# Two-layer latent backbone: attention norm weight, squares and high parts on ScalarE, norm product on GpSimd, and the last head's end in another order

## The chip, the cores and the metric

The kernel runs on one core of a Trainium2 chip. The metric is the device time of one execution in microseconds. A core has TensorE (PE in the profile; its weight loads are the row PEld), VectorE (DVE), ScalarE (ACT), GpSimd (POOL) and SyncE (SP), which issues nearly all DMAs from one queue. On-chip memory is SBUF; products land in PSUM, which has eight banks of 512 float32 columns here, and GpSimd is given no PSUM operand in this kernel.

## The reference

Two layers over 1024 latent tokens and 256 context tokens of 1024 channels: layer 0 is differential attention, layer 1 a state-space mixer, each followed by a squared-ReLU MLP, all in float32. The change touches layer 0's attention only:

```python
q_l = apply_rope(heads_qk(q_l), cos, sin) * scale          # 8 heads, 2 x 64 channels each
k_all, v_all = concatenate([k_c, k_l]), concatenate([v_c, v_l])   # 256 + 1024 keys
def attend(q, k, v):
    s = einsum('bqhcd,bkhcd->bhcqk', q, k)             # two maps c = 0, 1 per head
    p = softmax(s)
    w = p[:, :, 0] - lam * p[:, :, 1]
    o = einsum('bhqk,bkhe->bqhe', w, v)                    # 128 channels per head
    return rmsnorm(o, subln_g) * (1.0 - lambda_init)       # norm over the 128 channels, weight subln_g
y_lat = einsum('bte,ed->btd', o_l, w_o)                    # and y_ctx from the context alone
```

The context's queries read only the context's 256 keys.

## The kernel before

**Precision.** A float32 product is done as three matmuls on rounded halves: `mm3` (L132, L133, L134) multiplies high by high, high by low and low by high. The high part is a ScalarE copy into a rounded type, the low part the difference (`split`, L137 and L138; the low part on VectorE, or on GpSimd where so given).

**Phase B** (`phase_b`, about 220 to 876 us) does the attention of all eight heads. A head h has nine units: u = 0 is the 256 context queries, u = 1 to 8 are 128 latent queries each; step n = 9h + u. `with self.manual()` puts PE, VectorE, ScalarE and GpSimd in the order in which the program issues their instructions. SyncE's queue is not part of that: DMAs are placed by a scheduler once their operands are ready, and then run in the queue's order. In a unit:

- `scores` (L579): 18 matmuls (12 for u = 0) into PSUM columns 0 to 1279 and 1792 to 3071, for the two maps.
- `maxima` (L588 for u = 0, L592): VectorE copies the scores to SBUF with a running minimum.
- `exps` (L599, L602): ScalarE, in place, with the sum.
- `combine` (L610, L611, L613): VectorE, reciprocal, factor, and the difference of the two maps over 1280 columns (L613).
- In the next unit PE transposes the result (`w_part`, L620, L625) in parts w0 (four blocks), w1 (two), w2 (four). `w_direct` makes halves from PSUM: high on ScalarE (L631), low on VectorE (L632). `w_copy` frees PSUM first: a ScalarE copy to SBUF (L638), then high (L641) and low (L642) on GpSimd. The bank called `whole`, 1280 to 1791, shares banks with both maps' scores.
- Two units after an even u, `values` multiplies the halves of a pair of units by V into 256 columns of bank 6. `pair_out` copies the result (L732, ScalarE), squares it (L733, GpSimd, into `sq`), stores it to DRAM (`od`). `pair_sums` (L740) multiplies the squares by ones on PE.
- Between these PE works through `groups`: the q and k projections of the next head (`proj_group`; rotary product L534 on GpSimd, rotary add L537 on VectorE), and in head 7 the first part of the output product, `wo_group` (one 128-token tile over heads 0 to 5). A list of four numbers (`FILLS`, and for n from 63 on the tuple `a`) cuts the group's products into three fills between the other steps.
- **Norm.** At u 3 to 5 the statistics of the head before are finished (`norm_calc` L746 to L748, power on GpSimd L144, `norm_rows` writes rows `rsd`). At u 6, 7, 8 and the next head's 0, 1, `norm_load` brings one pair (values and broadcast row) from DRAM, and `norm_pair` in the same unit multiplies value, weight `self.sg` and row (L775, VectorE), splits it (ScalarE, GpSimd) and stores both halves (`on`). Two buffers take turns, for head 5 only one. For head 6 `norm6` (L796) does the same straight into the output product's operand `oT`; for head 7 `norm7` builds a diagonal matrix of the factors (L811, GpSimd), spreads it with ones on PE (L815) and multiplies (L817).
- **Turn to the output product.** From n = 62 `oT` takes the place of the projections' operand in the buffer H: `beside7` loads the stored halves of heads 0 to 5. `wload6` and `wsplit6` bring the output weights (n 57 to 62, and 72). `wo_group` (n 63 to 73) puts sums of six heads for each tile to DRAM (L858, `wod`); `wo_last` (n 74 to 76) does heads 6 and 7 for tiles 8, 9 and 0 to 4 into banks `WO_BANKS`, and the next phase does the rest.

In the main loop a unit takes one of two orders: with a pair to multiply that isn't pair 0 (or after u 0) the transposes come right after `values` (`late`; and `inside` where no group runs, u 4, 6, 8), otherwise there is a fill first.

Of the kernel before, what the change touches and what calls it, by code (L numbers as in the profile page):

```python
# [70 lines left out]
class Prog:  # L71
# [562 lines left out]
    def w_copy(self, tb, hi, lo):  # L634

        m, n = tb.shape[1:]
        t = shaped(self.wraw.next()[:, 0 : m * n], (m, n))
        self.nc.scalar.activation(t, tb, AF.Copy)  # L638

        def halves():  # L640
            self.nc.gpsimd.tensor_scalar(hi, t, 1.0, 0.0, ALU.mult, ALU.add)  # L641
            self.nc.gpsimd.tensor_tensor(lo, t, hi.bitcast(F32), ALU.subtract)  # L642

        return halves
# [7 lines left out]
    AHEAD = {0: (1, 0), 1: (1, 2), 2: (0, 2), 3: (1, 1), 5: (0, 0), 7: (0, 1)}  # L652
    FILLS = {0: (0, 4, 5, 8), 1: (0, 2, 2, 8), 2: (0, 2, 8, 8), 3: (0, 3, 7, 8)}

# [27 lines left out]
    def phase_b(self):  # L682
# [47 lines left out]
        def pair_out(h, pair):  # L730
            d = o7[pair % 2] if h == 7 else outs.next()
            nc.scalar.activation(d, pb[:, 0:256], AF.Copy)  # L732
            nc.gpsimd.tensor_tensor(sq, d, d, ALU.mult)  # L733
            if h < 7:
                self.dma(self.od[h, :, 256 * pair : 256 * pair + 256], d)

        def pair_sums(h, pair):
# [28 lines left out]
        def norm_load(h, pair):  # L766
            i = 1 if h == 5 else nbuf.next()
            nloaded.append(i)
            self.dma(nbufs[i][0], self.od[h, :, 256 * pair : 256 * pair + 256])
            self.dma(nbufs[i][1], self.rsd[h, 2 * pair : 2 * pair + 2].rearrange("a b -> (a b)").partition_broadcast(128))  # L770

        def norm_pair(h, pair):
            i = nloaded.pop(0)
            (nob, nrb), (nhi, nlo) = nbufs[i], nsplit[i]
            nc.vector.scalar_tensor_tensor(nob, nob, self.sg, nrb, ALU.mult, ALU.mult)  # L775

# [16 lines left out]
        def norm6(u):  # L793
            for (ob, rb), pair in zip(buf6, pairs6[u]):
                g, c0 = cols7[pair]
                nc.vector.scalar_tensor_tensor(ob, ob, self.sg, rb, ALU.mult, ALU.mult)  # L796
                self.split(self.oT[g][0][:, 6, c0 : c0 + 256], self.oT[g][1][:, 6, c0 : c0 + 256], ob, nc.gpsimd)
# [5 lines left out]
        def norm7(pair):  # L803
# [10 lines left out]
            def norm():  # L814
                mm(b, ones, diag.rearrange("p a b -> p (a b)"), start=True, stop=True)  # L815
                t = o7[pair % 2]
                nc.vector.scalar_tensor_tensor(t, t, self.sg, b, ALU.mult, ALU.mult)  # L817
                self.split(self.oT[g][0][:, 7, c0 : c0 + 256], self.oT[g][1][:, 7, c0 : c0 + 256], t, nc.gpsimd)
# [6 lines left out]
                 (((self.R, 0), (self.R, 4)), ((self.R, 8), (self.R, 12)), ((self.R1, 0), (self.R1, 4)), ((self.R, 36), (self.R, 40)))]  # L825
        wraw6 = [shaped(self.wv(x, 1024), (2, 512)) for x in (0, 0, 4)]

        def wload6(j):
            wo = self.I["attn_w_o"][0].rearrange("(k p) n -> p k n", p=128)
            self.dma(wraw6[j], wo[:, 2 * j : 2 * j + 2, 0:512])  # L830

        def wsplit6(j):
            hi, lo = wregs[j]
            self.split(hi, lo, self.wo_raws[0] if j == 3 else wraw6[j], nc.gpsimd)
            wt6.extend((hi[:, i], lo[:, i]) for i in range(2))
# [11 lines left out]
        def wo_group(i):  # L847
            g = 2 if i > 7 else i // 4
            c0 = 128 * (i - self.G_TILES[g][0])
            b = self.bank(i - 6 if 6 < i < 8 else 7)  # L850

            def product(k):
                hh, hl = (t[:, k, c0 : c0 + 128] for t in self.oT[g])
                return lambda: self.mm3(b, hh, hl, wt6[k][0], wt6[k][1], k == 0, k == 5)

# [4 lines left out]

            return [product(k) for k in range(6)], [out]

        def wo_last(*tiles):
            for i in tiles:
                g, b = 2 if i > 7 else i // 4, self.bank(self.WO_BANKS[i])
                c0 = 128 * (i - self.G_TILES[g][0])
                for k in (6, 7):
                    hh, hl = (t[:, k, c0 : c0 + 128] for t in self.oT[g])
                    self.mm3(b, hh, hl, wt6[k][0], wt6[k][1], k == 6, k == 7)

# [16 lines left out]
        with self.manual():  # L887
            for n in range(72 + 5):
# [27 lines left out]
                if groups:  # L916
                    if n < 63 or 0 < u < 3:
                        a = self.FILLS.get(u, (0, 2, 6, 8))
                    else:
                        a = (0, 4, 4, 6) if u == 0 else (0, 0, 3, 6) if late else (0, 2, 4, 6)  # L920
                    if n > 71:
# [15 lines left out]

                def copied(*ws):
                    for f in [self.w_copy(*w) for w in ws if w]:
                        f()  # L940

# [4 lines left out]
                def output(*a):  # L946
                    pair_out(*a)
                    sums.append((n + (parts != 1), lambda: pair_sums(*a)))
                    if a[0] == 7:
                        tail.append((n + 1, a[1]))  # L950

                def do_sums():
# [3 lines left out]
                def norm():  # L956
                    if front and n - 6 >= 9 and (n - 6) % 9 < 5 and (n - 6) // 9 < 7:
                        return norm_pair((n - 6) // 9 - 1, (n - 6) % 9)

                if late or parts == 1:  # L960
# [7 lines left out]
                    else:  # L968
                        if pv:
                            values(*pv)  # L970
                        if parts == 1:
                            fill(0)
# [6 lines left out]
                    if pv:  # L979
                        output(*pv)  # L980
                    if front:
                        self.combine(u, p, s0, sn)
                    split = norm()
                    if inside:
                        copied(w2, w1)
                    else:
                        direct(w0)
                        copied(w1)
                        if n != 73 and parts != 1:
                            fill(0)  # L990
                        fill(1)
# [3 lines left out]
                else:  # L995
                    if pv:
                        values(*pv)
                        output(*pv)
                    fill(0)
# [28 lines left out]
                if split:  # L1028
                    split()
                todo7, run7 = run7, []  # L1030
# [42 lines left out]
                if tail and tail[0][0] == n:  # L1073
                    run7.append(list(norm7(tail.pop(0)[1])))

# [1585 lines left out]
```

## Time and profile before

| | |
|---|---|
| median of 3 runs | 2837.14 us (2833.94 to 2844.83) |
| profiled execution | 2841.76 us, its span 2840.0 us |
| granted TensorE clock, mean | 0.988 |
| TensorE busy | 2717.6 us, 96% of the span |
| VectorE busy | 2034.9 us, 72% |
| ScalarE busy | 1368.8 us, 48% |
| GpSimd busy | 981.0 us, 35% |
| one head in the middle of phase B (head 3) | 76.3 us |

How to read the rows. A timeline row has the start, the duration, engine, line, operation, tiles written and read, their sizes, the count, and in brackets the idle time of the engine just before and what ended it. A group row has the count, busy time in us, mean ns, and idle time before with what ended it. The row of one line's instructions has count, shortest, median and longest ns, and first and last start. A row of stretches has from and to, the length, busy time of PE, PEld, DVE, ACT, POOL with counts, the clock, the DMA engines' busy share, and GB/s. In the chain of work that ended last each row is start, duration and what. A matmul's end is modelled, so a row's matmuls can overlap the next. L632 is line 632 of the kernel.

### The profile page before, as it was taken

How to read it: one execution, taken by the hardware profiler on the slowest of the kernel's cores; microseconds unless marked ns; L12 is line 12 of the kernel's file. 1: busy time of each engine (PE TensorE's matmuls, PEld its weight loads, DVE VectorE, ACT ScalarE, POOL GpSimd, SP SyncE). 2: the span in 40 equal slices, each digit the busy share in tenths (PEclk: the TensorE clock that was granted, in tenths of full speed). 3: DMA queues.
4: the chain of work that ended last, by engine and by line, in shares of the span. 5: the costliest groups of instructions: out<-in, count | busy, mean ns of one | idle time of the engine just before them, and what ended most of it. 6: DMA issues, size and time to landing. Idle time of an engine off the chain costs nothing.

```text
span 2840.0 us, 43822 instructions
## 1 busy us (share of the span) xinstructions
PE 2717.6 (96%) x15645; PEld 2257.1 (79%) x15645; DVE 2034.9 (72%) x3029; ACT 1368.8 (48%) x2589; POOL 981.0 (35%) x822
## 2 busy tenths in 40 slices
PE   6999999999899999999999999789999999999999
PEld 4687888888777788778877888788887778878887
DVE  6367888888764667666798877899533697668466
ACT  3425565666554743333444445577444633344443
POOL 3314556556554600000030013688122143235414
PEclk9999999999999999999999999899999999999999
DMA  9954232333516368885799977579642244476544
GB/s 275 322 171 137 66 90 89 94 94 118 171 48 191 119 212 301 301 302 198 275 309 296 289 226 245 182 233 313 217 164 82 71 164 160 152 251 223 168 132 141
DMA packets 377447, 539.12 MB, mean 190 GB/s; under 512 B 38286, under 2 KB 231052, under 8 KB 374028
## 3 DMA queue, kind: packets, MB, share of 16 engines
q1 hardware_dynamic: 377228, 536.32, 58.2%
q8 instruction: 123, 2.02, 0.3%
q14 instruction: 96, 0.79, 0.1%
HBM read 367.54 MB, written 164.47 MB: 187 GB/s over the span
## 4 chain that ended last, share of the span: by engine, by line
PE 55%; DVE 8%; DMA 6%; issue 3%; POOL 2%; ACT 2%; SPq 0%; DVEq 0%; POOLq 0%; ACTq 0%
PE PS L132 16%; PE PS L134 16%; PE PS L133 16%; PE PS L2010 2%; DMA FU<-in_mlp_w 2%; PE PS L2045 2%; DMA Ta<-FU 1%; DMA W<-in_mlp_w 1%; DVE R L138 1%; ACT F L602 1%; DVE H L138 1%; PE PS L579 1%; DVE FD L2019 1%; PE PS L2042 1%; PE PS L1319 0%
## 5 line engine op out<-in xcount | busy, mean ns | idle before, releaser
L132 PE MATMUL PS<-H 128*128 128x512 f32 x1072 | 421.4, 394 | 2.4 <-ACT H L137 2.1
L134 PE MATMUL PS<-H 128*128 128x512 f32 x1072 | 417.9, 390 | 1.9 <-DVE H L2336 1.3
L133 PE MATMUL PS<-H 128*128 128x512 f32 x1072 | 418.2, 390 | 0.0
L132 PE MATMUL PS<-H,R 128*128 128x512 f32 (+1 forms) x828 | 308.0, 374 | 4.1 <-ACT R L137 2.3
L134 PE MATMUL PS<-H,R 128*128 128x512 f32 (+1 forms) x828 | 297.6, 360 | 0.8 <-POOL R L138 0.8
L133 PE MATMUL PS<-H,R 128*128 128x512 f32 (+1 forms) x828 | 298.2, 360 | 0.0
L132 PEld LDWEIGHTS PS<-H 128*128 128x128 f32 x1072 | 201.7, 188 | 50.3 <-issue 6.1
L134 PEld LDWEIGHTS PS<-H 128*128 128x128 f32 x1072 | 201.4, 188 | 45.2 <-DVE H L2336 1.7
L133 PEld LDWEIGHTS PS<-H 128*128 128x128 f32 x1072 | 201.7, 188 | 40.9
L132 PE MATMUL PS<-R,H 128*128 128x512 f32 x534 | 213.6, 401 | 4.0 <-ACT H L137 3.3
L137 ACT ACTIVATE H<-U 128x640 fp32r<-128x640 f32 x216 | 131.8, 674 | 172.6 <-PE PS L133 143.2
L137 ACT ACTIVATE R<-W 128x512 fp32r<-128x512 f32 (+1 forms) x185 | 129.3, 706 | 176.7 <-PE PS L133 102.3
L602 ACT ACTIVATE F<-F,stat 128x1280 f32<-128x1280 f32 x128 | 174.1, 1361 | 82.7 <-DVE F L592 82.6
L134 PE MATMUL PS<-R,H 128*128 128x512 f32 x534 | 211.4, 397 | 1.8 <-DVE H L138 1.8
L133 PE MATMUL PS<-R,H 128*128 128x512 f32 x534 | 210.2, 394 | 0.1
L138 DVE TENSOR_TENSOR H<-U,H 128x640 fp32r<-128x640 f32 x216 | 167.1, 808 | 49.4 <-ACT H L137 48.7
L138 DVE TENSOR_TENSOR H<-W,H 128x512 fp32r<-128x512 f32 (+1 forms) x137 | 123.9, 915 | 103.6 <-ACT H L137 103.2
L592 DVE TENSOR_SCALAR_CACHE_REDUCE F<-PS 128x1280 f32<-128x1280 f32 x128 | 185.2, 1483 | 14.6 <-PE PS L579 14.1
L137 ACT ACTIVATE H<-W 128x512 fp32r<-128x512 f32 (+2 forms) x158 | 95.6, 613 | 188.9 <-PE PS L133 116.9
L132 PEld LDWEIGHTS PS<-H,R 128*128 128x128 f32 x828 | 156.9, 190 | 33.8 <-issue 4.1
L134 PEld LDWEIGHTS PS<-H,R 128*128 128x128 f32 x828 | 156.7, 189 | 26.4 <-POOL R L138 1.0
L133 PEld LDWEIGHTS PS<-H,R 128*128 128x128 f32 x828 | 157.1, 190 | 19.9
(530 smaller groups left out, 6718.7 us busy)
## 6 DMA issues: line engine op xcount, KB each, us to landing
W<-in_mlp_w SPq DMA_DIRECT2D x176, 256.0 KB, 3.3
U<-Aa SPq DMA_DIRECT2D x108, 320.0 KB, 3.8
Aa<-FU SPq DMA_DIRECT2D x91, 320.0 KB, 4.8
Ad<-F SPq DMA_DIRECT2D x112, 256.0 KB, 3.0
W<-Ad SPq DMA_DIRECT2D x112, 256.0 KB, 2.7
FU<-in_mlp_w SPq DMA_DIRECT2D x32, 512.0 KB, 5.8
Ta<-FU SPq DMA_DIRECT2D x16, 1024.0 KB
U<-in_ada_w SPq DMA_DIRECT2D x32, 512.0 KB, 9.3
```

The costliest lines, as they stand in the source:

```text
L132: mm(out, ah, bh, start=first, stop=False, **kw)
L133: mm(out, ah, bl, start=False, stop=False, **kw)
L134: mm(out, al, bh, start=False, stop=last, **kw)
L137: self.nc.scalar.activation(hi, src, AF.Copy)
L138: (lo_eng or self.nc.vector).tensor_tensor(lo, src, hi.bitcast(F32), ALU.subtract)
L579: self.nc.tensor.matmul(self.PS[:, o : o + n], Q[x][r, q0 : q0 + 128], K[y][r, k0 : k0 + n], start=i == 0, stop=i == 2)
L592: ts(p[c], self.PS[:, 1792 * c : 1792 * c + 1280], 1.0, None, ALU.mult, ALU.min, accum_out=sm[:, c : c + 1])
L602: nc.scalar.activation(p[c], p[c], AF.Exp, bias=sm[:, c : c + 1], scale=-1.0, accum_out=sn[:, 0:1] if c else s0[:, u + 1 : u + 2])
L2010: mm(b[:, o : o + 160], X[:, d, i, 64 * j : 64 * j + 128], U[:, 4 * n + i, cols], start=True, stop=True)
L2019: v.tensor_tensor(four(t), x, four(P), ALU.mult)
L2042: mm(o, U[:, 4 * n + i, 32:160], T[:, i], start=True, stop=False)
L2045: mm(o, cs[d][n % 2][j][:, i], W[:, d, i], start=False, stop=d == 1 and j == 1)
```

## The change

The norm weight `sg` becomes the scale of ScalarE's copy out of PSUM in `pair_out`, so the stored values have it already. The squares are taken by ScalarE from PSUM, unscaled, in a closure that the loop calls after the copies or right after the output. The norm products of `norm_pair` and `norm6` become a plain product on GpSimd; `norm7`'s on VectorE loses the weight. The high part in `w_copy` is a ScalarE copy. For head 5 the norm product runs one unit after its load, from the two buffers. The third split of output weights moves from the end of n 62 to the middle of n 63, its load from n 60 to n 61 into the one buffer that all use. Tile 8's group covers heads 0 to 3, and its other four heads go to the end. Fills are cut at other places; from n 63 to 71 the first fill comes ahead of the transposes. Tiles 6 and 7 use banks 4 and 1. At the end, pair 3's diagonal is made one step earlier, pair 4's before the products of tiles 8, 9 and 0, and tiles 1 to 4 follow in one step.

```diff
     def w_copy(self, tb, hi, lo):
         def halves():
-            self.nc.gpsimd.tensor_scalar(hi, t, 1.0, 0.0, ALU.mult, ALU.add)
+            self.nc.scalar.activation(hi, t, AF.Copy)
             self.nc.gpsimd.tensor_tensor(lo, t, hi.bitcast(F32), ALU.subtract)
...
-    FILLS = {0: (0, 4, 5, 8), 1: (0, 2, 2, 8), 2: (0, 2, 8, 8), 3: (0, 3, 7, 8)}
+    FILLS = {0: (0, 4, 6, 8), 1: (0, 2, 2, 8), 2: (0, 4, 8, 8), 3: (0, 3, 7, 8)}
...
         def pair_out(h, pair):
-            nc.scalar.activation(d, pb[:, 0:256], AF.Copy)
-            nc.gpsimd.tensor_tensor(sq, d, d, ALU.mult)
+            nc.scalar.activation(d, pb[:, 0:256], AF.Copy, scale=self.sg)
             if h < 7:
                 self.dma(self.od[h, :, 256 * pair : 256 * pair + 256], d)
+            return lambda: nc.scalar.activation(sq, pb[:, 0:256], AF.Square)
...
         def norm_load(h, pair):
-            i = 1 if h == 5 else nbuf.next()
+            i = nbuf.next()
...
         def norm_pair(h, pair):
-            nc.vector.scalar_tensor_tensor(nob, nob, self.sg, nrb, ALU.mult, ALU.mult)
+            nc.gpsimd.tensor_tensor(nob, nob, nrb, ALU.mult)
...
         def norm6(u):
-                nc.vector.scalar_tensor_tensor(ob, ob, self.sg, rb, ALU.mult, ALU.mult)
+                nc.gpsimd.tensor_tensor(ob, ob, rb, ALU.mult)
...
             def norm():
-                nc.vector.scalar_tensor_tensor(t, t, self.sg, b, ALU.mult, ALU.mult)
+                nc.vector.tensor_tensor(t, t, b, ALU.mult)
...
         def wo_group(i):
-            b = self.bank(i - 6 if 6 < i < 8 else 7)
+            b, last = self.bank({6: 4, 7: 1}.get(i, 7)), 3 if i == 8 else 5
...
         def wo_last(*tiles):
-                for k in (6, 7):
+                k0 = 4 if i == 8 else 6
+                for k in range(k0, 8):
...
-                        a = self.FILLS.get(u, (0, 2, 6, 8))
+                        a = self.FILLS.get(u, (0, 1, 5, 8))
                     else:
-                        a = (0, 4, 4, 6) if u == 0 else (0, 0, 3, 6) if late else (0, 2, 4, 6)
+                        a = (0, 4, 4, 4) if u == 0 else (0, 2, 5, 6) if late else (0, 2, 4, 6)
...
                 def norm():
-                    if front and n - 6 >= 9 and (n - 6) % 9 < 5 and (n - 6) // 9 < 7:
-                        return norm_pair((n - 6) // 9 - 1, (n - 6) % 9)
+                    m = n - 7 if n > 59 else n - 6
+                    if front and m >= 9 and m % 9 < 5 and m // 9 < 7 and n != 60:
+                        return norm_pair(m // 9 - 1, m % 9)
...
-                        if parts == 1:
+                        if parts == 1 or 62 < n < 72:
                             fill(0)
...
                     if pv:
-                        output(*pv)
+                        square = output(*pv)
+                        if not inside:
+                            square()
...
                     if inside:
-                        copied(w2, w1)
+                        h2, h1 = copy(w2), copy(w1)
+                        square()
+                        h2()
+                        h1()
...
-                        output(*pv)
+                        output(*pv)()
...
-                    copied(w2)
+                    h2 = copy(w2)
                     if front:
                         self.combine(u, p, s0, sn)
                     fill(2)
                     direct(w1)
+                    h2()
...
+                if n == 63:
+                    wsplit6(2)
...
                 if n == 74:
-                    run7.append(list(norm7(tail.pop(0)[1])))
-                    wo_last(8, 9)
+                    diagonals, f = norm7(tail.pop(0)[1])
+                    diagonals()
+                    run7.append([f])
+                    wo_last(8, 9, 0)
+                    todo7 = []
+                else:
+                    todo7, run7 = run7, []
...
-                if n in (58, 61, 62, 72):
-                    wsplit6((58, 61, 62, 72).index(n))
-                if n in (57, 58, 60):
-                    wload6((0, 1, 2)[(57, 58, 60).index(n)])
+                if n in (58, 61, 72):
+                    wsplit6((58, 61, 63, 72).index(n))
+                if n in (57, 58, 61):
+                    wload6((57, 58, 61).index(n))
...
-                    wo_last(*((0,), (1,), (2, 3, 4))[n - 74])
+                    wo_last(*((), (1, 2, 3, 4), ())[n - 74])
...
-                    run7.append(list(norm7(tail.pop(0)[1])))
+                    f = list(norm7(tail.pop(0)[1]))
+                    if n == 72:
+                        f.pop(0)()
+                    run7.append(f)
```

More of the change, by code (lines that the diff above doesn't have):

```diff
@@ L825, in phase_b @@
                  (((self.R, 0), (self.R, 4)), ((self.R, 8), (self.R, 12)), ((self.R1, 0), (self.R1, 4)), ((self.R, 36), (self.R, 40)))]
-        wraw6 = [shaped(self.wv(x, 1024), (2, 512)) for x in (0, 0, 4)]
+        wraw6 = shaped(self.wv(0, 1024), (2, 512))
         def wload6(j):
             wo = self.I["attn_w_o"][0].rearrange("(k p) n -> p k n", p=128)
-            self.dma(wraw6[j], wo[:, 2 * j : 2 * j + 2, 0:512])
+            self.dma(wraw6, wo[:, 2 * j : 2 * j + 2, 0:512])
         def wsplit6(j):
             hi, lo = wregs[j]
-            self.split(hi, lo, self.wo_raws[0] if j == 3 else wraw6[j], nc.gpsimd)
+            self.split(hi, lo, self.wo_raws[0] if j == 3 else wraw6, nc.gpsimd)
             wt6.extend((hi[:, i], lo[:, i]) for i in range(2))
@@ L849, in wo_group @@
             c0 = 128 * (i - self.G_TILES[g][0])
-            b = self.bank(i - 6 if 6 < i < 8 else 7)
+            b, last = self.bank({6: 4, 7: 1}.get(i, 7)), 3 if i == 8 else 5
             def product(k):
                 hh, hl = (t[:, k, c0 : c0 + 128] for t in self.oT[g])
-                return lambda: self.mm3(b, hh, hl, wt6[k][0], wt6[k][1], k == 0, k == 5)
+                return lambda: self.mm3(b, hh, hl, wt6[k][0], wt6[k][1], k == 0, k == last)
             def out():
@@ L859, in out @@
                 self.dma(self.wod[i], wsum)
-            return [product(k) for k in range(6)], [out]
+            return [product(k) for k in range(last + 1)], [out]
         def wo_last(*tiles):
@@ L866, in wo_last @@
                 c0 = 128 * (i - self.G_TILES[g][0])
-                for k in (6, 7):
+                k0 = 4 if i == 8 else 6
+                for k in range(k0, 8):
                     hh, hl = (t[:, k, c0 : c0 + 128] for t in self.oT[g])
-                    self.mm3(b, hh, hl, wt6[k][0], wt6[k][1], k == 6, k == 7)
+                    self.mm3(b, hh, hl, wt6[k][0], wt6[k][1], k == k0, k == 7)
         wo_at = dict(zip((63, 64, 65, 66, 68, 69, 70, 71, 72, 73), [8, 9] + list(range(8))))
@@ L936, in direct, with copied, copy @@
                         self.w_direct(*w)
-                def copied(*ws):
-                    for f in [self.w_copy(*w) for w in ws if w]:
-                        f()
+                def copied(w):
+                    copy(w)()
+                def copy(w):
+                    return self.w_copy(*w) if w else lambda: None
                 def exps(c):
@@ L946, in output @@
                 def output(*a):
-                    pair_out(*a)
+                    square = pair_out(*a)
                     sums.append((n + (parts != 1), lambda: pair_sums(*a)))
@@ L950, in output @@
                         tail.append((n + 1, a[1]))
+                    return square
                 def do_sums():
@@ L988, in phase_b @@
                         copied(w1)
-                        if n != 73 and parts != 1:
-                            fill(0)
                         fill(1)
@@ L1029, in phase_b @@
                     split()
-                todo7, run7 = run7, []
                 if n == 74:
-                    run7.append(list(norm7(tail.pop(0)[1])))
-                    wo_last(8, 9)
+                    diagonals, f = norm7(tail.pop(0)[1])
[5 more added lines that the diff above has]
+                    todo7, run7 = run7, []
                 for f in todo7:
```

## The prediction

> **What bounds the kernel now.** I read the page first, then busy time by stretch, then who waits for whom, then the order of time around each wait. Units are named by head h and unit u, n = 9h + u.
>
> ```profile
> span 2840.0 us, 43822 instructions
> PE 2717.6 (96%) x15645; PEld 2257.1 (79%) x15645; DVE 2034.9 (72%) x3029; ACT 1368.8 (48%) x2589; POOL 981.0 (35%) x822
> ```
>
> TensorE (PE) is the bound, so the change can only gain where PE stands still, and only in phase B, the stage it touches (about 220 to 876 us). Busy time there: one middle head (3), the turn from head 6 to head 7 (n 62 to 64), head 7, and the end.
>
> ```profile
> 445.96:522.28 76.32, 73.66 (x533) 63.16 (x533) 67.26 (x107) 46.78 (x95) 44.50 (x42) 1.00 0.29 89
> 744.91:779.13 34.22, 27.44 (x165) 23.08 (x163) 20.94 (x40) 16.22 (x35) 16.18 (x15) 0.80 0.53 165
> 779.13:837.34 58.21, 54.89 (x365) 44.67 (x366) 44.05 (x70) 31.00 (x60) 29.77 (x32) 1.00 0.16 54
> 837.34:876.02 38.68, 33.70 (x169) 26.80 (x167) 14.72 (x28) 11.47 (x24) 16.70 (x22) 0.96 0.38 122
> ```
>
> The columns are length, then busy PE, weight loads, VectorE (DVE), ScalarE (ACT), GpSimd (POOL), granted clock. PE idles 2.7 us in a middle head, 6.8 at the turn (with the clock at 0.80), 3.3 in head 7 and 5.0 at the end. The waits of head 3 by releaser:
>
> ```profile
> PE PS L625 <- DVE R L632: 1.4, 3, 0.9
> PE PS L132 <- DVE R L632: 0.7, 1, 0.7
> ...
> ```
>
> Total, times, longest: most of the 2.7 is VectorE's low parts L632. What stands in front of them, at u 0:
>
> ```profile
> 519.78 1.82 DVE L613 SCALAR_TENSOR_TENSOR F<-F,stat 128x1280 f32<-128x1280 f32 x1
> 521.53 0.83 DVE L775 SCALAR_TENSOR_TENSOR W<-W,lamc 128x256 f32<-128x256 f32 x1
> 522.28 0.41 DVE L588 TENSOR_SCALAR_CACHE_REDUCE F<-PS 128x256 f32<-128x256 f32 x1
> 523.66 0.68 DVE L632 TENSOR_TENSOR R<-PS,R 128x512 fp32r<-128x512 f32 x1
> 521.75 0.63 PE L625 MATMUL PS<-ident,F 128*128 128x128 f32 x4
> 522.14 0.48 PE L132 MATMUL PS<-H,R 128*128 128x512 f32 x1
> 522.91 0.60 PE L625 MATMUL PS<-ident,F 128*128 128x128 f32 x4
> 524.39 0.44 PE L625 MATMUL PS<-ident,F 128*128 128x128 f32 x2 [0.88 <-DVE R L632]
> ```
>
> The norm product L775 stands right ahead of the maxima L588 and of L632. Four transposes that nothing holds are followed after 0.39 (521.75 to 522.14), here after 1.48: the wait costs 1.09, 0.2 more than the 0.88 shown idle, because ends are modelled. At u 7 (and u 2) it is L613, stretched by GpSimd:
>
> ```profile
> 477.17 1.55 DVE L613 SCALAR_TENSOR_TENSOR F<-F,stat 128x1280 f32<-128x1280 f32 x1
> 477.25 1.95 POOL L641 TENSOR_SCALAR R<-F 128x512 fp32r<-128x512 f32 x1 [7.16 <-ACT F L638]
> 509.96 2.68 DVE L613 SCALAR_TENSOR_TENSOR F<-F,stat 128x1280 f32<-128x1280 f32 x1
> 510.00 1.29 POOL L642 TENSOR_TENSOR R<-F,R 128x512 fp32r<-128x512 f32 x1
> 513.03 0.39 PE L132 MATMUL PS<-R 128*128 128x256 f32 x1 [0.69 <-DVE R L632]
> ```
>
> L613 takes 1.55 when it is first and 2.68 when GpSimd is at work as it starts; the second time it lost 1.13, about L642's length. [...]
>
> At the turn, in the chain of waits, then PE, GpSimd and the clock:
>
> ```profile
> 744.47 6.42 DMA H<-on
> 750.91 5.13 DMA F<-rsd
> 756.13 0.88 DVE F L775
> ...
> 759.71 0.69 PE L625 MATMUL PS<-ident,F 128*128 128x128 f32 x2 [6.66 <-DVE R L632]
> 751.76 1.27 POOL L534 TENSOR_TENSOR FC<-FC,W 128x512 f32<-128x512 f32 x1 [3.45 <-DMA FC<-FC]
> 760.00:765.00 5.00, 4.88 (x16) 3.73 (x16) 4.86 (x9) 2.83 (x9) 2.79 (x3) 0.50 0.42 112
> ```
>
> The norm product of head 5 waits on VectorE for a row load queued behind the H loads; maxima, L632 and PE wait behind it, 6.66 us, and PE then runs at half clock.
>
> **The change part by part.** Durations (min/median/max ns in the rows with counts; the group row gives busy us, mean ns):
>
> ```profile
> L641 POOL TENSOR_SCALAR R<-F 128x512 fp32r<-128x512 f32 (+1 forms) x88 | 100.0, 1136 | 99.8 <-ACT F L638 99.6
> L733 POOL TENSOR_TENSOR adat<-FC x23: 611/615/1785, 239.5 to 861.4; 128x256 f32<-128x256 f32 x23
> L138 POOL TENSOR_TENSOR F<-F x17: 729/742/1191, 361.9 to 778.2; 128x256 fp32r<-128x256 f32 x17
> L732 ACT ACTIVATE FC<-PS x23: 362/368/386, 236.7 to 861.0; 128x256 f32<-128x256 f32 x23
> L599 ACT ACTIVATE F<-F,stat x20: 493/496/499, 370.6 to 677.4; 128x256 f32<-128x256 f32 x20
> L137 ACT ACTIVATE R<-W x30: 613/616/1073, 226.1 to 855.4; 128x512 fp32r<-128x512 f32 x26, 128x1024 fp32r<-128x1024 f32 x4
> ```
>
> *High parts to ScalarE.* [...] 40 squares enter at L732's 0.37, 15 us, and 40 L733 leave GpSimd. A head gets 11 copies and 5 squares, so ScalarE in head 3 goes from 46.8 by about 9 to 56 of 76 us: no bound. Its queue matters more. High parts and squares are issued behind the copies that free PSUM, so the copy L638, on which PE's next scores wait, moves only where the square precedes the exps (u 2, 0.37); the cover is ScalarE's idle time, 30 us a head, which lies at the start of the next unit. The weight in L732's scale costs between 0 and 0.13 (L599, as wide and with an operand per partition, less L732); I take 0.1, on the path at u 4, 6 and 8. [...]
>
> *Norm product to GpSimd.* 30 L775 (0.83 above) and 5 L796 leave VectorE; 35 products of 0.62 to 0.74 (L733, L138) enter GpSimd, 26 us, whose queue has lost over 100. Behind a late one wait, on GpSimd, the unit's low parts and, on ScalarE, the norm's high part and whatever follows it.
>
> *Fill lists.* The same products of PE at other places in the unit: 0 in themselves. With one product less ahead of it (u 5, 7) the first transpose comes earlier and must find the bank read by the square; that is issued right behind the two copies, so 0, and 0.4 if it were late.
>
> *Middle heads.* At u 0 the wait is 1.09. L775 gone is 0.83, L613 back from 1.82 to 1.55 is 0.27, and the fill list gives PE one more product there: all goes. At u 7 it is 0.69 idle, 0.9 with the 0.2; the low part now starts after ScalarE's high part, so L613 is first (1.55) and ends over 1 us earlier: 0.9 goes. What is left of the 2.7 is 1.1 in four small waits of u 2 to u 4, with 0.2 each an estimated 1.9. There the low part follows L613 and then holds VectorE's rotary add and norm sums, so I take 0.6 of 0 to 1.9. Sum 2.6 per head, bounds 1 to 3.9; heads 1 to 6 have five full sets, 13, and the ends of heads 0, 1 and 6 about 1: **14**, bounds 5 to 20.
>
> *The turn.* For head 5 the norm comes one unit after its load, from two buffers in place of one, and on GpSimd. Moved with it, per pair: one product, one ScalarE high part (under 0.62), one low part (0.74) and two stores on the SP queue; the weight split of n 62 (1.07 on ScalarE, L137's longest, and its low part on GpSimd) goes to n 63 and its 512 KB load from n 60 to 61, behind H loads. VectorE no longer waits, so 6.66 goes. Late next: L534 on GpSimd starts at 751.76 on its own DMA, the product of pair 1 follows to about 753.8, and ScalarE's norm high part stands in front of n 63's L631; so L632 ends near 755.5 (753.8 and three times about 0.6), not 759.7. After that PE has no fill left in n 63 (0,4,4,4) and waits for L638, which has four exps of 0.50 (L599) ahead of it, about 1.5. Also tile 8's copy now waits for the split's low part (same W buffer), on ScalarE ahead of n 64's exps; PE has about 9 us of work a unit there (27.44 in three), so I cost it nothing, and 2 without that cover. The scores of n 64 come 6 earlier. The half clock cost 4 to 5 more (three units took 34.2 for 27.4 of work, itself stretched); I take 0.5 of it, because about 4 us of idle in two pieces stay. Bounds 3 to 11, taken **6.5**.
>
> *Head 7 and the end.*
>
> ```profile
> 820.77 0.33 PE L625 MATMUL PS<-ident,F 128*128 128x128 f32 x1 [1.45 <-DVE R L632]
> 833.44 2.38 DVE L796 SCALAR_TENSOR_TENSOR W<-W,lamc 128x256 f32<-128x256 f32 x2
> 838.89 0.33 PE L625 MATMUL PS<-ident,F 128*128 128x128 f32 x1 [0.65 <-DVE F L592]
> 840.30 0.33 PE L625 MATMUL PS<-ident,F 128*128 128x128 f32 x1 [0.97 <-DVE F L592]
> 840.00:845.00 5.00, 4.47 (x16) 3.17 (x17) 3.41 (x7) 2.77 (x7) 2.67 (x3) 0.66 0.00 0
> 848.10 0.50 PE L132 MATMUL PS<-R,H 128*128 128x512 f32 x1 [0.69 <-ACT W L858]
> 870.42 0.48 PE L815 MATMUL PS<-FC 128*128 128x256 f32 x1 [1.66 <-POOL FC L811]
> ```
>
> n 69 and 71 now run two products before the transposes that waited: 1.0 of 1.45 and all of 0.65 + 0.97. With L796 (2.38 for two) off VectorE the maxima also come earlier. The clock drop at 840 to 845 (0.34 of 5 us, 1.7) goes in part, 0.9. Other banks for tiles 6 and 7 remove the 0.69. The last diagonals are made while PE does tiles 8, 9 and 0, so 1.66 goes. Tile 8's two products moved to the end are PE work moved, 0. Sum 5.9, plus 0.6 for small waits: **6.5**, bounds 3 to 8.
>
> On the clock: two waits of under 1 us at 838.89 and 840.30 came ahead of the drop in the row 840 to 845, so I let the turn's two pieces of 2.5 and 1.5 us cost it too. [...]
>
> Sum 14 + 6.5 + 6.5 = 27. The profiled execution took 2841.76, so 2814.8; the median 2837.14 is 4.6 lower, so 2810.1. Later stages take over any shift: their first work waits for PE's last product here, and their loads for buffers.
>
> **The rivals.** (1) *The port wait only moves.* If GpSimd keeps getting in ahead of L613, the norm product on GpSimd holds VectorE off for 0.74 where L775 took 0.83, and low parts still collide with L613. Then the middle heads give nothing: 27 - 14 = 13, 2824. [...] For it: 2.68 beside L642. Against: L613 starts before the low part once the high part is made behind L631. (2) *The turn keeps its wait*, on ScalarE and GpSimd behind the same slow loads, and the half clock: it gives 0 to 3, 2814 to 2817. For it: L534's 3.45 wait. (3) *PE's idle time stays as it is*: new waits on ScalarE eat the 27, 2837. Against: ScalarE's 30 idle us per head. (4) *Slower*: low parts of the weights arrive late. At u 7 L642 ends at 511.29 and the products of values start at 513.03, 1.7 later, and at u 3 and 5 it is alike; from 2 us of delay PE waits, and with 3 us more at each, 3 x 3 x 6 = 54 less 27 gives 2864. Against: the high part follows L631 by 0.6, and L641 often took 1.9 itself.
>
> **How the numbers follow.** Forecast 0.56, (1) 0.16, (2) 0.15, (3) 0.09, (4) 0.04. About 0.5%, 14 us, is what a measurement of this kernel tells from no change. Faster by more: forecast, (2) and two thirds of (1), 0.82; within: 0.14; slower 0.04. All lower bounds of the gains add to 5 + 3 + 3 = 11 (2826), all upper ones to 20 + 11 + 8 = 39 (2798); the runs' own spread (2833.94 to 2844.83) adds some below: 2794 to 2827, which takes in (1) and (2).
>
> **What would show it.** In the changed profile a middle head should take 73 to 74.5 us, L613 near 1.55 at u 7, no wait at u 0; between the maxima of n 62 and n 65 27 to 29 us; GpSimd's L641 gone, ScalarE near 1440 us. Wrong if PE's waits name ScalarE's high parts or GpSimd's product, or if the clock still halves for 13 us at the turn.

## The result and the profile after

The changed kernel takes 2807.57 us (median of 5 runs, 2805.7 to 2812.76) against 2840.46 (5 runs, 2833.94 to 2844.83): a ratio of 0.9891, 95% interval 0.9876 to 0.9905. A later series gave 2810.87 (5 runs) against 2838.84: 0.9898, 0.9884 to 0.9911. The page of the profiled execution (2805.7 us) of the changed kernel:

```profile
span 2803.9 us, 43710 instructions
PE 2702.6 (96%) x15645; PEld 2251.9 (80%) x15645; DVE 2000.8 (71%) x2994; ACT 1420.8 (51%) x2717; POOL 900.0 (32%) x729
```

The stretches that answer to the four of before (a middle head; n 62 to 64; head 7 to n 70; the end), with the same columns: from and to, length, the five busy times, then the granted clock:

```profile
440.75:513.36 72.61, 72.39 (x532) 63.12 (x531) 62.00 (x102) 52.78 (x112) 36.37 (x30) 1.00 0.32 96
726.23:751.86 25.63, 23.38 (x171) 20.21 (x170) 17.44 (x37) 18.12 (x41) 15.10 (x13) 1.00 0.65 202
751.86:808.85 56.99, 53.40 (x349) 42.88 (x350) 39.43 (x66) 35.22 (x70) 22.45 (x24) 1.00 0.20 63
808.85:846.67 37.82, 34.97 (x191) 29.02 (x189) 13.16 (x26) 14.30 (x31) 15.82 (x22) 1.00 0.35 117
```

The whole span by the starts of units (a unit starts with its first maxima), with a second execution of the changed kernel (profiled at 2810.87; its span 2809.1) beside the first:

| us | before | changed | changed, second | gain, predicted |
|---|---|---|---|---|
| up to the first unit | 220.33 | 221.95 | 222.01 | -1.6, -1.7; 0 |
| heads 0 to 6 up to n 62 | 524.58 | 504.28 | 505.04 | 20.3, 19.5; **14** |
| the turn, n 62 to 64 | 34.22 | 25.63 | 28.24 | 8.6, 6.0; **6.5** |
| n 65 to the next phase's first product | 96.89 | 94.81 | 96.43 | 2.1, 0.5; **6.5** |
| the rest | 1964.0 | 1957.2 | 1957.4 | 6.8, 6.6; 0 |

Phase B gives 31.0 and 26.0, where 27 were predicted; two of its three terms were wrong, in opposite directions. The rest isn't the change's as far as can be seen: its code is the same in all fourteen traces of this study, and it takes 1956.9 to 1967.7 in them, 1958.5 to 1964.0 in the three with the heads of before. Most of the first execution's 6.8 may be the clock: the rest of before holds twelve windows of 3.41 us at a clock of 0.50 (the end of the span left out), that of the first changed execution nine, and three such windows cost up to 5.1.

In the middle head a single wait of PE is left:

```profile
PE PS L740 <- ACT F L638: 0.2, 1, 0.2
```

L613 (count, busy time, mean ns, idle before), first before, then changed, from 300 to 700 us:

```profile
L613 DVE SCALAR_TENSOR_TENSOR F<-F,stat 128x1280 f32<-128x1280 f32 x42 | 82.2, 1956 | 1.5
```
```profile
L613 DVE SCALAR_TENSOR_TENSOR F<-F,stat 128x1280 f32<-128x1280 f32 x44 | 69.6, 1582 | 1.5
```

And at u 7, in the timeline of the changed kernel, the order is the one predicted: L613 is first with 1.55 and GpSimd's low part beside it takes 2.02, where before they took 2.68 and 1.29.

```profile
502.63 1.55 DVE L613 SCALAR_TENSOR_TENSOR F<-F,stat 128x1280 f32<-128x1280 f32 x1
503.31 2.02 POOL L642 TENSOR_TENSOR R<-F,R 128x512 fp32r<-128x512 f32 x1 [1.59 <-ACT R L641]
```

### The profile page after: what moved, and what is told of

Its sections match the earlier page's. It is cut to its first block, busy times and chain, and to the rows that moved or that the text cites. A ratio compares the mean times of both kernels' runs of the same rounds, so it can differ in the third digit from the quotient of the medians.

```text
span 2803.9 us, 43710 instructions
## 1 busy us (share of the span) xinstructions
PE 2702.6 (96%) x15645; PEld 2251.9 (80%) x15645; DVE 2000.8 (71%) x2994; ACT 1420.8 (51%) x2717; POOL 900.0 (32%) x729
## 3 DMA queue, kind: packets, MB, share of 16 engines
q8 instruction: 123, 2.02, 0.3%
## 5 line engine op out<-in xcount | busy, mean ns | idle before, releaser
L642 POOL TENSOR_TENSOR R<-F,R 128x512 fp32r<-128x512 f32 (+1 forms) x88 | 119.3, 1367 | 209.9 <-ACT R L641 144.9
L132 PEld LDWEIGHTS PS<-H,R 128*128 128x128 f32 x828 | 156.9, 190 | 33.4 <-issue 4.1
L134 PEld LDWEIGHTS PS<-H,R 128*128 128x128 f32 x828 | 156.7, 189 | 26.4 <-POOL R L138 1.1
```

The lines of the kernel that those rows point to most:

```text
L132: mm(out, ah, bh, start=first, stop=False, **kw)
L134: mm(out, al, bh, start=False, stop=last, **kw)
```

## Experiments

**The heads.** Four runs undo one part each of the changed kernel, one undoes two, one does one part alone on the kernel before. First the high parts:

```diff
-            self.nc.scalar.activation(hi, t, AF.Copy)
+            self.nc.gpsimd.tensor_scalar(hi, t, 1.0, 0.0, ALU.mult, ALU.add)
```

> The changed kernel with one part undone: the high part of w_copy (L641) is made on GpSimd again, all else as changed. Port theory (the step of the prediction for u 7): GpSimd works again while L613 starts, so L613 is stretched to 2 us or more at u 7, the wait of 0.7 to 0.9 at u 7 comes back and the small waits of u 2 to u 4 (another 1 or so) with it: a middle head takes 74.0 to 74.9 us against 72.6 to 72.9, and the whole 8 to 13 us more than the changed kernel, 2815 to 2821. Rival, fills: PE was only short of products at the right place, and the new fill lists gave them; then a head stays within 0.3 of 72.7 and the time within 3 of 2807.6.

2824.7 us (ratio 0.9938, 0.9921 to 0.9955). Head 3, and L613:

```profile
442.81:517.66 74.85, 73.30 (x533) 63.12 (x532) 64.13 (x103) 48.18 (x100) 46.44 (x42) 1.00 0.29 90
```
```profile
L613 DVE SCALAR_TENSOR_TENSOR F<-F,stat 128x1280 f32<-128x1280 f32 x43 | 75.1, 1746 | 1.5
```

2.2 of the head's 3.7 and 0.16 of L613's 0.37 come back; u 0, 2 and 4 have waits of 0.35 to 0.42 again, u 3 has two of 0.17 and 0.23. The size is the theory's, and the rival (fills alone) falls. "Port", here and in the first rival of the prediction, is a name for L613's stretch beside GpSimd's work (2.68 in place of 1.55 at u 7 of before); what causes the stretch no run shows. The place isn't the one expected: at u 7 L613 takes 1.87 and PE doesn't wait. L613 is longer at u 2 (2.68) and at u 0 (its two small ones take 0.93 and 1.61, 0.48 in the changed kernel).

The norm product back on VectorE:

```diff
-            nc.gpsimd.tensor_tensor(nob, nob, nrb, ALU.mult)
+            nc.vector.tensor_tensor(nob, nob, nrb, ALU.mult)
```

> The changed kernel with the norm product of norm_pair (L775) on VectorE again, now as a plain product of 128x256 without the weight. Prediction's step for u 0: L775 stands in front of the maxima again, 0.6 to 0.8 each; the wait at u 0 was 1.09, of which the new fill list covers one product (about 0.4), so 0.3 to 0.8 of it comes back per head: a head takes 73.0 to 73.6 and the whole 2 to 6 us more, 2810 to 2814. At the turn the product comes one unit after its load, so VectorE does not wait there: n 62 to n 65 stays within 1 of 25.6. Rival, fills: one product more at u 0 covers all, a head stays within 0.2 of 72.7. [...]

2807.84 us (0.9886, 0.9872 to 0.9901), and the head

```profile
441.55:514.49 72.94, 72.71 (x533) 63.56 (x532) 62.43 (x107) 53.26 (x111) 30.86 (x26) 1.00 0.31 93
```

against 72.61 to 72.91 in heads 2 to 5 of the changed kernel: nothing. The expected 0.3 to 0.8 missed; the rival with the fill was right so far.

The fill lists of n below 63 as before:

```diff
-    FILLS = {0: (0, 4, 6, 8), 1: (0, 2, 2, 8), 2: (0, 4, 8, 8), 3: (0, 3, 7, 8)}
+    FILLS = {0: (0, 4, 5, 8), 1: (0, 2, 2, 8), 2: (0, 2, 8, 8), 3: (0, 3, 7, 8)}
...
-                        a = self.FILLS.get(u, (0, 1, 5, 8))
+                        a = self.FILLS.get(u, (0, 2, 6, 8))
```

> The changed kernel with the fill lists of heads 0 to 6 (n below 63) as before: (0, 4, 5, 8) at u 0, (0, 2, 8, 8) at u 2, (0, 2, 6, 8) at u 5 and 7. A head took 76.3 before, 72.7 changed, 74.9 with the high part back on GpSimd and 72.9 with the norm product back on VectorE, so of the 3.6 the high part holds 2.1 and 1.4 is open. Theory fills: a product more behind the transposes of u 0 covers L632, which the norm product on VectorE then no longer costs; with the old lists a wait of 0.3 to 1 comes back at u 0 and a head takes 73.2 to 74.1, the whole 3 to 9 us more. Rival: with L775 and the squares gone from their queues nothing waits at those places, the lists bring 0 and a head stays within 0.2 of 72.7; the open 1.4 is then the squares'.

2811.95 us (0.9912, 0.9896 to 0.9929); head 3 takes 73.47, heads 4 and 5 73.65: the lists hold 0.8 (in head 2, with 72.96, only 0.35).

The squares back on GpSimd:

```diff
-            return lambda: nc.scalar.activation(sq, pb[:, 0:256], AF.Square)
+            return lambda: nc.gpsimd.tensor_tensor(sq, d, d, ALU.mult)
```

> The changed kernel with the square on GpSimd again, taken from the copy in SBUF (which has the norm weight in it here, so the statistics are those of weighted values). GpSimd gets 40 products of about 0.62 back, ScalarE loses 40 of about 0.38. Theory: nothing waits for the squares but L740 two steps later, 0 to 0.3 per head, within 2.5 of 2807.6. [...]

2814.79 us (0.9924, 0.9905 to 0.9943); heads 73.02 to 73.24, so 0.3 to 0.6, over the theory's 0 to 0.3; part of the 7 us is the rest of the span, 1967.7 here, the longest of all. Of the head's 3.5 to 3.7, the high parts hold 2.2, the lists 0.8, the squares 0.4, the norm product 0.

That left open whether the product costs nothing or is hidden by the list. Both undone together:

> The changed kernel with both the fill lists of n below 63 as before and the norm product of norm_pair back on VectorE. Alone, the lists cost 0.4 to 0.8 a head (73.0 to 73.7 against 72.6 to 72.9) and the norm product 0 (72.9). The prediction put the wait of 1.09 at u 0 down to the norm product in front of the maxima. If that holds and the new list only hides it, both together bring back more than the sum: a wait of 0.8 to 1.1 at u 0 and a head of 74.0 to 74.7, 6 to 11 us more than the changed kernel. Rival: the wait at u 0 was L613's, held up by the high parts on GpSimd, and the product never was on the path: then both together are the sum, 73.0 to 73.8.

2815.25 us (0.9917, 0.9899 to 0.9935), heads 73.60 to 73.67: the sum. At u 0 the product stands where it stood before, right ahead of the maxima, and is harmless:

```profile
513.83 1.55 DVE L613 SCALAR_TENSOR_TENSOR F<-F,stat 128x1280 f32<-128x1280 f32 x1
515.30 0.42 DVE L775 TENSOR_TENSOR W<-W 128x256 f32<-128x256 f32 x1
515.39 2.17 POOL L642 TENSOR_TENSOR R<-F,R 128x512 fp32r<-128x512 f32 x2 [3.47 <-ACT R L641]
...
518.30 0.44 PE L625 MATMUL PS<-ident,F 128*128 128x128 f32 x2 [0.28 <-DVE R L632]
```

The wait of 0.28 is also there with the old lists alone. So of the 0.88 shown idle at u 0 before, 0.60 is gone with the product (now without the weight) still in its place, and the new list covers the other 0.28. No run takes the product alone out of the kernel before; what it cost there by itself stays open.

The high part alone, put on the kernel before (the first diff, reversed):

> The kernel before with one part alone: the high part of w_copy (L641) on ScalarE, right behind the copy, nothing else. Undone in the changed kernel it cost 2.0 to 2.2 a head. Port theory: GpSimd's work at the start of L613 goes, L613 falls from a mean of 1.96 to 1.7 or less, and a head takes 74.0 to 74.9 in place of 76.3; with six heads 8 to 14 us less than before. Rival: the high part stands behind L638 and ahead of L631 and the exps on ScalarE in the old order, which makes these 0.6 later, and a head stays within 0.5 of 76.3.

2831.05 us (0.9968, 0.9956 to 0.998); head 3 takes 75.65, so 0.7 and not 2.2: neither the theory's 74.0 to 74.9 nor the rival's. At u 7 L613 takes 1.55 and the wait halves (0.20 and 0.17 in place of 0.69), but u 0 gets worse:

```profile
518.28 0.61 POOL L733 TENSOR_TENSOR adat<-FC 128x256 f32<-128x256 f32 x1 [1.97 <-ACT FC L732]
518.35 1.89 DVE L613 SCALAR_TENSOR_TENSOR F<-F,stat 128x1280 f32<-128x1280 f32 x1
519.55 2.70 POOL L642 TENSOR_TENSOR R<-F,R 128x512 fp32r<-128x512 f32 x2 [0.66 <-POOL adat L733]
520.16 1.50 DVE L775 SCALAR_TENSOR_TENSOR W<-W,lamc 128x256 f32<-128x256 f32 x1
...
523.70 0.44 PE L625 MATMUL PS<-ident,F 128*128 128x128 f32 x2 [1.55 <-DVE R L632]
```

The square starts 0.07 before L613, which loses 0.34 (1.89 for 1.55); then the low part gets in ahead of the product, which takes 1.50 where the shortest of before takes 0.47. With lists and product undone (above), GpSimd at u 0 was idle for the 3.47 up to 515.39, and L613 and the product took 1.55 and 0.42. The parts aren't additive: the high part is worth 0.7 with the squares on GpSimd and the old order, 2.2 without.

**The turn.** Alone on the kernel before, with the weight still in VectorE's product:

```diff
-            i = 1 if h == 5 else nbuf.next()
+            i = nbuf.next()
...
+                    m = n - 7 if n > 59 else n - 6
+                    if front and m >= 9 and m % 9 < 5 and m // 9 < 7 and n != 60:
+                        return norm_pair(m // 9 - 1, m % 9)
...
+                if n == 63:
+                    wsplit6(2)
...
```

> The kernel before with the turn's part alone: for head 5 two buffers and the norm product one unit after its load, still on VectorE with the weight; the third weight split in n 63 with its load in n 61, tile 8's group cut to heads 0 to 3. Prediction's step: VectorE does not wait for the row load, 6.66 goes, of the 34.2 us from n 62 to n 65 6.5 go (27.7), with some half clock left. Rival, the clock by windows: in both traces each stretch of half clock begins at one and the same spacing of 3.41 us and follows a window of that length in which PE was busy for less than about half; two waits near 1 us leave 0.64 busy and no drop, and 8 to 9 go (25.5 to 26.5). Rival, the product must be off VectorE: the wait moves to L613 or the maxima and 0 to 3 go. Middle heads stay at 76.3 by all three. Time: before less 6.5, 8.5 or 0 to 3.

2836.92 us (0.9983, 0.9972 to 0.9993). The stretch, and what is late in it:

```profile
746.40:775.03 28.63, 23.56 (x162) 20.43 (x161) 22.11 (x39) 16.25 (x35) 16.72 (x15) 0.94 0.52 168
...
759.73 2.35 POOL L138 TENSOR_TENSOR R<-W,R 128x1024 fp32r<-128x1024 f32 x1
759.82 2.53 DVE L613 SCALAR_TENSOR_TENSOR F<-F,stat 128x256 f32<-128x256 f32 x1
762.75 0.39 PE L132 MATMUL PS<-R 128*128 128x256 f32 x1 [2.45 <-DVE R L632]
```

5.6 go. The rest is L613 beside GpSimd again: the weight split's low part (2.35) starts 0.09 before a small L613, which takes 2.53 (0.48 in the changed kernel). Most of the 5.6 is given back behind n 65, where 96.89 become 100.61: tile 8's two products have moved there (six matmuls, 0.23 apart in the changed kernel's trace: 1.4), and two waits are longer, that for L632 in n 71 (1.67 in place of 0.23) and that for L811 (2.45 in place of 1.66). Before has one window at a clock of 0.50 in this stretch (3.41 at 841.22).

The reverse, the changed kernel with product and load in one unit:

```diff
-                    m = n - 7 if n > 59 else n - 6
-                    if front and m >= 9 and m % 9 < 5 and m // 9 < 7 and n != 60:
+                    m = n - 6
+                    if front and m >= 9 and m % 9 < 5 and m // 9 < 7:
```

> The changed kernel with head 5's norm product in the same unit as its load, two buffers, on GpSimd. Second rival of the prediction (the turn keeps its wait on GpSimd and ScalarE): the product waits for the row load, ScalarE's high part of the norm waits for it, and L631 and L638 stand behind on ScalarE; n 62 to n 65 takes 31 to 35 instead of 25.6 (28.3 where a half clock falls in) and the whole 4 to 8 us more. Rival: with the product off VectorE and two buffers the load is early enough or nobody waits for GpSimd, 25.6 to 28.5 and within 2 of 2807.6.

2813.2 us (0.9915, 0.99 to 0.9929); n 62 to n 65 takes 29.53, less than expected, at a clock of 0.88. The changed kernel takes 25.63 there, and 28.24 in an execution with the same clock of 0.88 (below), so the shift by one unit is worth 3.9 or 1.3. In n 63:

```profile
736.55 0.72 POOL L775 TENSOR_TENSOR F<-F 128x256 f32<-128x256 f32 x1
737.31 0.42 ACT L137 ACTIVATE F<-F 128x256 fp32r<-128x256 f32 x1 [3.87 <-POOL F L775]
737.63 0.58 ACT L631 ACTIVATE R<-PS 128x512 fp32r<-128x512 f32 x1
...
738.99 0.69 PE L625 MATMUL PS<-ident,F 128*128 128x128 f32 x2 [3.14 <-DVE R L632]
```

That is the second rival's chain (GpSimd's product late, ScalarE's high part behind it, L631 behind that), half as long as on VectorE (3.14 in place of 6.66).

**Head 7 and the end.** The changed kernel with head 6's product back on VectorE:

```diff
-                nc.gpsimd.tensor_tensor(ob, ob, rb, ALU.mult)
+                nc.vector.tensor_tensor(ob, ob, rb, ALU.mult)
```

> The changed kernel with head 6's norm product alone (L796, five of them at n 69 to 71) on VectorE again, without the weight. Theory for the new wait in n 70 (2.04 us for L632, and 0.6 for L740): ScalarE's high part of the second norm pair waits for GpSimd, which has two diagonals, two products and two low parts in a row, and L631 is queued behind it on ScalarE. With the products on VectorE, which has nothing to do for 3.4 us there, both high parts come early: 2.0 to 2.6 go, n 70 takes 9.7 to 10.3 instead of 12.26, and the time is 2 to 3 below the changed kernel's. [...]

2803.31 us (0.9867, 0.9851 to 0.9884). First the changed kernel's new wait in n 70 and the whole of n 70, then n 70 with the product on VectorE:

```profile
799.91 0.73 POOL L796 TENSOR_TENSOR W<-W 128x256 f32<-128x256 f32 x1
800.67 0.42 ACT L137 ACTIVATE H<-W 128x256 fp32r<-128x256 f32 x1 [1.53 <-POOL W L796]
800.99 0.58 ACT L631 ACTIVATE R<-PS 128x512 fp32r<-128x512 f32 x1
...
802.35 0.44 PE L625 MATMUL PS<-ident,F 128*128 128x128 f32 x2 [2.04 <-DVE R L632]
...
796.59:808.85 12.26, 9.62 (x60) 7.43 (x60) 7.95 (x13) 6.27 (x13) 7.35 (x10) 1.00 0.28 83
```
```profile
797.15:808.23 11.08, 10.72 (x71) 8.68 (x71) 9.13 (x16) 6.38 (x13) 6.93 (x9) 1.00 0.25 83
```

n 70 falls from 12.26 to 11.08, short of the expected 10.3 since PE also does 1.1 more work in it; from n 65 to the next phase 94.81 become 91.96. The cause of the wait is shown, for this order of the fills: ScalarE's high part waited for GpSimd's product, and L631 stood behind it.

The end as before (fills from n 63, banks, diagonals, the steps of tiles 0 to 4):

```diff
-                        a = (0, 4, 4, 4) if u == 0 else (0, 2, 5, 6) if late else (0, 2, 4, 6)
+                        a = (0, 4, 4, 6) if u == 0 else (0, 0, 3, 6) if late else (0, 2, 4, 6)
...
-                        if parts == 1 or 62 < n < 72:
+                        if parts == 1:
...
```

> The changed kernel with the end as before: from n 63 on the fills cut as before and the first fill behind the transposes, tiles 6 and 7 in their old banks, the last two diagonals made where they were, tiles 0 to 4 in their old steps (tile 8's cut to heads 0 to 3 stays). The prediction gave these edits 5.9. From n 65 to the first product of the next phase the changed kernel gained only 1 to 2, and 2.6 of waiting came new at n 70, which the norm product on GpSimd causes and this run keeps. Theory: the edits bring 3 to 5, and the new wait took them back: the waits at n 69 (1.45), at the ends (0.65, 0.97), of L858 (0.69) and of L815 (1.66) return, 2810 to 2813. Rival: the edits bring nothing by themselves (waits only move), within 1.5 of 2807.6.

2815.05 us (0.9922, 0.9905 to 0.9939), somewhat over the expected range. From n 65 to n 71, and from there to the next phase:

```profile
750.55:806.87 56.32, 53.43 (x349) 42.89 (x350) 39.33 (x67) 35.29 (x70) 22.46 (x24) 1.00 0.20 64
806.87:848.60 41.73, 36.75 (x191) 30.31 (x189) 12.89 (x26) 14.53 (x31) 15.70 (x22) 0.96 0.31 104
```

The edits are worth 3.9 at the end (where this run's clock is 0.96, in the second row) and cost 0.7 up to n 71: 3.2 of the predicted 5.9. This run doesn't keep the new wait, as expected of it: in n 70 PE waits 0.66 for L632 though the product is on GpSimd, and n 71 has a wait of 2.15 for L632 (0.94 in the changed kernel). So the 2.04 in n 70 takes both, the product on GpSimd and the new order, and the 3.2 is what the edits hold with that wait taken off. Of the waits named, those for L858 (0.69), L811 (1.36) and at n 69 (0.76) return; the two for the maxima don't.

**The clock, and a better version.** The changed kernel again, unaltered:

> The changed kernel once more, beside the runs above. If the half clock at the turn depends on how the windows of 3.41 us fall on the two waits of n 63, this profile shows n 62 to n 65 at either 25.6 or 28.3 with the same waits, and middle heads at 72.6 to 72.9 as before; the median lies at 2805 to 2811. Rival: the turn always takes 25.6 in this kernel and the 28.3 of the run with head 6's norm product on VectorE had another cause.

The same two waits, and 28.24 in place of 25.63, n 70 13.77 (at a clock of 0.76) in place of 12.26. First three neighbouring stretches of 3.4 us of this run, then the two of the first execution in which the same waits fell:

```profile
735.50:738.90 3.40, 1.43 (x11) 0.95 (x9) 2.16 (x7) 2.81 (x10) 1.37 (x3) 1.00 0.98 298
738.90:742.30 3.40, 3.12 (x14) 2.73 (x16) 2.84 (x7) 2.54 (x6) 2.31 (x2) 0.50 0.52 183
742.30:745.70 3.40, 3.40 (x19) 2.99 (x18) 1.98 (x3) 0.93 (x3) 2.44 (x2) 0.50 0.13 39
```
```profile
733.90:737.30 3.40, 2.21 (x14) 1.52 (x13) 2.30 (x8) 2.03 (x8) 2.15 (x3) 1.00 0.94 243
737.30:740.70 3.40, 2.34 (x22) 2.06 (x22) 3.03 (x8) 3.32 (x9) 1.53 (x2) 1.00 0.87 298
```

One window with both waits (PE busy for 1.43 of 3.4) is followed by 6.8 us at 0.50; the same waits in two windows (2.21 and 2.34) aren't. The turn and what follows up to the next phase make 4.2 of the 5.2 us between the spans of these two executions.

Head 6's product on VectorE, and at n 63 two of tile 8's products behind the first transposes:

```diff
-                        a = (0, 4, 4, 4) if u == 0 else (0, 2, 5, 6) if late else (0, 2, 4, 6)
+                        a = (0, 2, 4, 4) if u == 0 else (0, 2, 5, 6) if late else (0, 2, 4, 6)
```

> The changed kernel with head 6's norm product on VectorE (which alone gave 2803.3) and, at n 63, tile 8's four products cut as two before the first transposes and two behind them, in place of four before them. In n 63 PE waited 0.98 for L632 and 1.28 for L638, and where a window of 3.41 us caught both, 6.8 us of half clock followed and n 62 to n 65 took 28.3 in place of 25.6. Theory: the transposes come 1.5 earlier, L631, L632 and L638 with them; the waits fall to 0.3 and 1.1 or less, no window is half idle, n 62 to n 65 takes 24.5 to 25.5 in every run, and the median is 1 to 3 below 2803.3. Rival: L638 stands behind the four exps, which wait for the maxima and not for PE; then L740's wait grows by what L632's loses, and n 62 to n 65 stays at 25.6 or 28.3.

2805.14 us (4 runs, 2799.66 to 2807.02; 0.9879, 0.9866 to 0.9893), beside 2810.87 for the changed kernel in the same series. In its one profiled execution the waits in n 63 fall to 0.25 and 1.08, and the clock is whole:

```profile
726.63:751.34 24.71, 23.37 (x171) 20.11 (x170) 17.71 (x36) 18.12 (x41) 15.13 (x13) 1.00 0.65 205
```

The other cut of the fills is worth 0.9 at full clock (25.63 before it). From n 62 to the next phase it takes 116.65 where the changed kernel took 120.44 and 124.67; behind n 65 it takes 91.94, as with head 6's product alone (91.96). The stretches show the gain; the times' intervals still overlap, and 2803.3 wasn't undercut.

## Why the prediction came out as it did

**Middle heads: 14 predicted, 20.3 and 19.5 measured**, at the edge of its bounds. Heads 1 to 5 gave 16.7 and 16.5, put at 13; heads 0 and 6 gave 3.7 and 3.0, put at about 1. Of these 2.8 lie in head 6, which before has the waits of u 0 and u 2 to u 4 like the others. The range "73 to 74.5" for a head was missed by 0.1 to 0.4 (72.6 to 72.9 in heads 2 to 5 of the first execution). Right: u 7 (L613 at 1.55, wait gone; but no single part undone brings that wait back), no wait at u 0, ScalarE no bound (1420.8; 1440 foretold, 1368.8 with 88 copies of 0.62 and 40 squares of 0.37), the scale's 0.1 (L732 went from 370 to 462 ns).

The step that failed in its cause is the one at u 0: "L775 gone is 0.83". The run with the new lists and L775 back shows 0. GpSimd's rows at u 0 of before:

```profile
519.65 0.61 POOL L733 TENSOR_TENSOR adat<-FC 128x256 f32<-128x256 f32 x1 [1.92 <-ACT FC L732]
520.23 1.86 POOL L641 TENSOR_SCALAR R<-F 128x512 fp32r<-128x512 f32 x1
```

The square starts 0.13 before L613 (519.78, 1.82 in place of 1.55), and the high part is at work when L775 starts (521.53, 0.83 in place of the 0.47 of the shortest). So 0.36 of the 0.83 came only beside GpSimd's work.

The step that failed in size is that of u 2 to u 4, "I take 0.6 of 0 to 1.9": of the 1.1 shown idle there 0.23 is left, so about 0.9 went. I had kept most of it back because the low part would hold VectorE's rotary add and norm sums. In head 3 the rotary add of u 2 is longer beside it (L537 takes 1.45, before 0.68; L642 at work from 464.09 for 2.16, L537 from 465.35), but no wait of PE hangs on that, and the norm sum L746 falls from 1.03 to 0.33.

In the pairs of rows shown here, one instruction of VectorE and one of GpSimd, the one that starts first keeps its short time and the other is longer: L613 1.55 and L641 1.95 (477.17 and 477.25 of before), L733 0.61 and L613 1.89 (518.28 and 518.35 with the high part alone). One doesn't fit: at u 7 of before L613 starts 0.04 ahead of L642 by the record (509.96 and 510.00) and takes 2.68, L642 1.29. I weighed this stretch as a rival that would take the gain away, where the high parts' leaving GpSimd gave 2.2 of a head's 3.7.

**The turn: 6.5 predicted, 8.6 and 6.0 measured.** L632 was put 10.6 behind the maxima of n 62 (755.5 less 744.91); in the changed kernel it ends at 736.59 after 726.23, 10.4. The wait for L638 was put at 1.5 and is 1.28. The changed kernel's timeline:

```profile
735.27 0.60 ACT L631 ACTIVATE R<-PS 128x512 fp32r<-128x512 f32 x1 [1.71 <-PE PS L625]
735.90 0.69 DVE L632 TENSOR_TENSOR R<-PS,R 128x512 fp32r<-128x512 f32 x1 [0.98 <-ACT R L631]
736.64 0.44 PE L625 MATMUL PS<-ident,F 128*128 128x128 f32 x2 [0.98 <-DVE R L632]
...
738.36 0.61 PE L740 MATMUL PS<-lamc,adat 128*128 128x1 f32 x4 [1.28 <-ACT F L638]
```

Wrong was "about 4 us of idle in two pieces", which are 0.98 and 1.28, and with it the half clock: it comes in one of the two executions (6.8 us at 0.50) and not in the other (1.00). The "27 to 29 us" for the stretch held in the second alone (25.63 and 28.24). About 1.4 of the gain isn't one: tile 8's two products were moved out of this stretch and into the next, which I booked as 0 in both places.

**Head 7 and the end: 6.5 predicted, 2.1 and 0.5 measured.** The single waits went as said (n 69, the maxima at 838.89 and 840.30, L858, L815), but in the first execution n 71 has new ones of 0.94 and 0.62 for L632 and 0.51 for L817. Tile 8's two products take 1.4 in this stretch. The failing step is that of L796: I priced only that "off VectorE the maxima also come earlier" and put its new place on GpSimd at nothing, which cost 2.9 (94.81 against 91.96), and 4.5 in the second execution (96.43), whose n 70 ran at a clock of 0.76. I had named the rule myself, for the norm's pairs ("behind a late one wait, on GpSimd, the unit's low parts and, on ScalarE, the norm's high part and whatever follows it"), but didn't apply it to `norm6`, whose high parts stand ahead of the next unit's L631. The order edits held 3.2 of 5.9, with the wait that they and the product make together taken off.

**Rivals.** (1) fell. (2) happens in half measure without the shift by one unit (29.53 at the turn, 34.22 before). (3) and (4) fell: at u 7 L642 ends at 505.33 and no wait of PE names it. That the sum came within 4 of both executions is luck: two errors of 4 to 6 cancel.

## What to carry over

An instruction's duration in a trace may contain a stretch beside another engine's work (here L613 1.55 or 2.68, L775 0.47 or 1.50): before pricing a move by it, look for the same shape where GpSimd is idle, and ask of each GpSimd instruction what VectorE starts right after it. A step moved to another engine brings along what stands behind its consumer in that engine's queue (here L631, with 2.04 of PE's time in n 70); follow the order to the next unit's first copy. And with waits of 1 to 2 us close together, look at several executions: with the same two waits the turn took 25.63 in one of them and 28.24, at a clock of 0.88, in another.

## What the runs showed of the hardware

In the trace of before and the first one of the changed kernel the half clock (0.50) starts on one grid of 3.413 us and lasts whole multiples of it (3.41, 6.83, 13.65) except at the end of the span (3.98 and 3.55). Taken over the windows of this grid at full clock (the first 50 and last 30 us left out), a half window followed in 15 of 15 where PE's records cover under 0.425 of the window, in 1 of 9 from 0.425 to 0.6 (that from 837.80 of before, covered to 0.52), and in none of the 1552 above. What decides between 0.425 and 0.6 stays open. At the turn the first execution of the changed kernel had the full clock (and gained 8.6), the second 0.88 (and gained 6.0). The forecast's reasoning, from two waits and the drop at 841 of before, doesn't hold: the same two waits cost the clock in one execution and not in the other. In these executions the drop goes with the sum of idle time in one window, not with the number of waits.
